# Attention inside a decoder layer: the softmax of each head group cut into six stages, the transposes and products behind it at later weight halves

## The chip, the cores and the metric

The kernel runs on one core of one Trainium2 chip. The metric is the device time of one execution in microseconds (us). Engines are called as in the profile: PE (matmuls; PEld is its weight load), DVE (vector), ACT (scalar activations and copies), POOL and SP (which issues the weight loads).

## What is computed

One decoder layer over 256 tokens of width 2048 in float32: a normalisation, a wide input projection, two token mixers side by side (a recurrent one and attention), their merge, and an MLP. The change touches the attention alone: 32 query heads in 4 groups of 8, each group with one key and value head of 64 columns, a window of 128 tokens in blocks of 128, and one sink per head that takes part in the softmax.

```python
def sliding_window_sink_attention(q, k, v, sinks):
    ...
    scores = jnp.einsum('bnqhgd,bnkhd->bnhgqk', qb, kk).astype(jnp.float32)
    ...
    scores = jnp.where(valid, scores, NEG_INF)
    m = jnp.maximum(jnp.max(scores, axis=-1, keepdims=True), sink)
    p = jnp.exp(scores - m)
    denom = jnp.sum(p, axis=-1, keepdims=True) + jnp.exp(sink - m)
    probs = (p / denom).astype(v.dtype)
    out = jnp.einsum('bnhgqk,bnkhd->bnqhgd', probs, vv)
    return out.reshape(B, S, N_Q_HEADS * HEAD_DIM)
```

## The kernel before

All weights come through one stream (class `Stream`). A chunk of 128x2048 is loaded in two **halves** of 128x1024 (`wraw`, line 76). Each half is split in two float32r parts: ACT casts it to `whi` (line 94), and DVE subtracts that from the original to get `wlo` (line 95). There are 4 raw buffers and 6 of each part, and the split runs 6 halves ahead of the half that PE works on (`AHEAD`). A product takes three matmuls, high by high, low by high and high by low.

For each group `g` of heads there are two passes of PE over the normalised input `hT`, 8 halves each, 12 matmuls of 512 columns per half (`b_pass512`, lines 294, 296, 298): the **g pass** for a gate (banks `g`), then the **q pass** for the queries (banks `q0`, `q1`). The attention of a group is a generator (`attention`, line 532) that the next passes drive: `pump()` runs it up to its next `yield`. `b_pass512` pumps after every `every` halves: the g pass with `every=1`, so 8 times, the q pass with the default 2, so 4 times. The last group has no passes of heads behind it and is driven by the recurrent branch (`a_pair`, lines 254 and 256, tiles `ps`), four times in each pass of four halves. There the wide matmuls have 512 columns and the narrow ones 256.

The generator's stages, in order: rotary embedding of the queries and their transposes for the token blocks 0 and 1 (three stages, tiles `qr`, `pq`, `qT`); the scores; the softmax of block 0; in the next stage that of block 1; then the transposes of the probabilities of block 0 (`turn_probs(0)`, line 604, banks `pt`, copied out by ACT, line 606), an empty stage, those of block 1, and last the outputs (line 630, banks `po`, split by ACT and DVE into `yatt`, lines 634 and 635).

The scores (line 560, banks `sc`) are written in three parts: block 0 with 128 keys per query, and block 1 with 256 keys in two parts `j` = 0 and 1, each in two banks. A bank is emptied by DVE, which scales and masks (line 566, `s`), and then takes the row maxima (line 568, `stat`). In groups 0 to 2 the three parts have banks of their own; in the last group both parts of block 1 use the two banks of pool `psb`, so that the second part waits until the first has been masked. The softmax (lines 571 to 588) takes the maximum with the sink, negates it (575 to 577), computes the exponents on ACT with their sums (line 582, one instruction per head and block), and scales on DVE (lines 584, 585, 587, one instruction for each tile of 512 columns).

A scheduler turns the written order into one static order per engine; matmuls that are wrapped in `pin` keep the order in which they are written among each other. Each engine works off its list strictly in that order, as far as the weight loads of PE are left aside.

## Time and profile before

| | |
|---|---|
| median of 3 runs | 1512.85 us (1512.64 to 1513.12) |
| the profiled execution, its own time | 1512.09 us |
| its span, first to last instruction | 1510.3 us |
| mean granted clock of PE | 0.998 |
| idle time of all engines before the transposes of line 604, put down to the scaling of line 587 | 4.8 us in 5 places |
| casts `whi` (line 94) | 523, mean 1053 ns |
| subtractions `wlo` (line 95) | 523, mean 1221 ns |

In a timeline a row is: start, duration (both us), engine, line, operation, out<-in, shape, count, and in square brackets the idle time of the engine before it with what ended it. Rows with a count merge instructions that follow each other, and then the duration runs from the start of the first to the end of the last. Instructions of one engine overlap a little, so that the distance between two starts is shorter than a duration; where times are added up, starts are used.

The groups follow each other in the trace like this: the q pass of group 1 begins at 106.69 us with group 0's attention beside it, that of group 2 at 160.39 with group 1's, that of group 3 at 215.43 with group 2's, and the recurrent branch at 244.67 with group 3's. The times below that are called those of group 0, 1, 2 or 3 are those of the group whose attention runs. The products with the attention's output (`pp`) begin at 301.24.

### The profile page before, as it was taken

To read this page: it belongs to the slowest core of one execution; us is meant where nothing else is said; L and a number is where in the kernel's file an instruction comes from. 1 tells how busy PE (TensorE), PEld (TensorE's weight loads), DVE (VectorE), ACT (ScalarE), POOL (GpSimd) and SP (SyncE) were. 2 spreads that over 40 slices of the span, in tenths; PEclk is the share of its full clock that TensorE was granted. 3 is DMA by queue.
4 is the path that set the end of the run, shared out by engine and by line. 5 is a ranking of instruction groups with operands and counts; after the bars stand their busy time and mean duration, and the time that the engine had idled before them with its cause. 6 is when DMAs were issued, how large, how long until landed. Compare 5 with 4: busy or idle time off the path is not lost.

```text
span 1510.3 us, 20013 instructions
## 1 busy us (share of the span) xinstructions
PE 1492.1 (99%) x7600; PEld 1260.9 (83%) x7600; DVE 1102.4 (73%) x1379; ACT 829.6 (55%) x1143; POOL 1.7 (0%) x9
## 2 busy tenths in 40 slices
PE   9999999999999999999999999999999999999997
PEld 7887778788888888888888888888888888888886
DVE  6666677858669967555667866698886666789897
ACT  6554654647556766444345655465554555555453
POOL 0000000000000000000000000000000000000000
PEclk9999999999999999999999999999999999999999
DMA  6645445465646565555764756566667665576665
GB/s 254 222 141 188 141 131 172 153 195 167 213 166 212 175 206 196 189 191 187 277 216 140 265 188 193 192 196 213 212 203 237 195 193 188 187 239 210 203 216 187
DMA packets 83327, 296.19 MB, mean 196 GB/s; under 512 B 9760, under 2 KB 10016, under 8 KB 82208
## 3 DMA queue, kind: packets, MB, share of 16 engines
q1 hardware_dynamic: 79920, 287.58, 57.4%
q10 hardware_dynamic: 3312, 7.35, 1.3%
q8 instruction: 59, 0.97, 0.3%
q14 instruction: 36, 0.29, 0.1%
HBM read 288.60 MB, written 6.29 MB: 195 GB/s over the span
## 4 chain that ended last, share of the span: by engine, by line
PE 94%; DVE 4%; ACT 1%; issue 0%; DVEq 0%; ACTq 0%
PE ps L256 22%; PE ps L254 11%; PE dQ L1084 9%; PE s L1084 5%; PE dP L1084 4%; PE pp L294 4%; PE pp L298 4%; PE pp L296 4%; PE dCs L1084 3%; PE g L294 3%; PE g L298 3%; PE g L296 3%; PE q L296 2%; PE q L298 2%; PE q L294 2%; PE o L294 2%
## 5 line engine op out<-in xcount | busy, mean ns | idle before, releaser
L94 ACT CAST whi<-wraw 128x1024 fp32r<-128x1024 f32 x523 | 545.3, 1053 | 566.4 <-PE ps L256 132.3
L95 DVE TENSOR_TENSOR wlo<-wraw,whi 128x1024 fp32r<-128x1024 f32 x523 | 632.7, 1221 | 301.8 <-ACT whi L94 297.9
L256 PE MATMUL ps<-h2T,whi 128*128 128x512 f32 x960 | 223.9, 390 | 0.0
L256 PEld LDWEIGHTS ps<-h2T,whi 128*128 128x128 f32 x960 | 178.3, 188 | 35.5
L256 PE MATMUL ps<-hT,whi 128*128 128x512 f32 x512 | 121.3, 392 | 0.0
L254 PEld LDWEIGHTS ps<-h2T,wlo 128*128 128x128 f32 x960 | 119.2, 192 | 2.3
L254 PE MATMUL ps<-h2T,wlo 128*128 128x256 f32 x960 | 119.9, 283 | 0.0
L256 PEld LDWEIGHTS ps<-hT,whi 128*128 128x128 f32 x512 | 94.7, 188 | 20.1 <-issue 1.5
L1084 PE MATMUL dQ<-whi,uT 128*128 128x512 f32 x288 | 107.0, 389 | 0.0
L294 PE MATMUL g<-whi,hT 128*128 128x512 f32 x256 | 101.3, 396 | 0.0
L296 PE MATMUL g<-wlo,hT 128*128 128x512 f32 x256 | 100.2, 391 | 0.1
L298 PE MATMUL g<-whi,hT 128*128 128x512 f32 x256 | 99.9, 390 | 0.0
L254 PE MATMUL ps<-hT,wlo 128*128 128x256 f32 x512 | 64.9, 284 | 0.0
L254 PEld LDWEIGHTS ps<-hT,wlo 128*128 128x128 f32 x512 | 63.8, 192 | 1.2
L1084 PEld LDWEIGHTS dQ<-whi,uT 128*128 128x128 f32 x288 | 54.1, 188 | 11.2
L294 PEld LDWEIGHTS g<-whi,hT 128*128 128x128 f32 x256 | 48.1, 188 | 10.5 <-issue 1.0
L298 PEld LDWEIGHTS g<-whi,hT 128*128 128x128 f32 x256 | 48.1, 188 | 10.1
L296 PEld LDWEIGHTS g<-wlo,hT 128*128 128x128 f32 x256 | 48.2, 188 | 9.9 <-DVE wlo L95 0.5
L1084 PE MATMUL dQ<-wlo,uT 128*128 128x512 f32 x144 | 56.1, 390 | 0.0
L1084 PE MATMUL dP<-whi,uT 128*128 128x512 f32 x144 | 54.1, 390 | 0.0
L1084 PE MATMUL dCs<-whi,uT 128*128 128x512 f32 x144 | 54.1, 389 | 0.0
L130 DVE TENSOR_TENSOR tlo<-t,thi 128x1536 fp32r<-128x1536 f32 x28 | 49.2, 1756 | 6.4 <-ACT thi L129 6.4
(285 smaller groups left out, 2459.1 us busy)
## 6 DMA issues: line engine op xcount, KB each, us to landing
wraw<-in_w_up SPq DMA_DIRECT2D x128, 512.0 KB, 4.1
wraw<-in_w_dn SPq DMA_DIRECT2D x128, 512.0 KB, 4.7
wraw<-in_w_g SPq DMA_DIRECT2D x64, 512.0 KB, 4.5
wraw<-in_w_xy SPq DMA_DIRECT2D x64, 512.0 KB, 4.5
wraw<-in_w_q SPq DMA_DIRECT2D x32, 512.0 KB, 3.6
wraw<-in_w_ap SPq DMA_DIRECT2D x32, 512.0 KB, 4.7
wraw<-in_w_rp SPq DMA_DIRECT2D x32, 512.0 KB, 4.6
wraw<-in_w_out SPq DMA_DIRECT2D x32, 512.0 KB, 5.0
```

The source lines that it names most:

```text
L94: self.pin(self.nc.scalar.copy(hi, src))
L95: self.pin(self.nc.vector.tensor_tensor(lo, src, hi.bitcast(F32), ALU.subtract))
L130: v.tensor_tensor(lo, t, hi.bitcast(F32), ALU.subtract)
L254: mm(ps[:, f, 1, :], w, a[:, 0, :], start=False, stop=j == 1 and k == 7)
L256: mm(ps[:, f].rearrange("p a b -> p (a b)"), w, a.rearrange("p a b -> p (a b)"), start=kt == 0, stop=j == 3 and k == 7)
L294: mm(banks[tb][n], a[:, 0, t], hi[:, n * 512 : n * 512 + 512], start=first, stop=False)
L296: mm(banks[tb][n], a[:, 0, t], lo[:, n * 512 : n * 512 + 512], start=False, stop=False)
L298: mm(banks[tb][n], a[:, 1, t], hi[:, n * 512 : n * 512 + 512], start=False, stop=last)
L1084: mm(b, a[x], w[y], start=not begun and i == 0, stop=tail and i == 2)
```

## The change

Three things change. The masks and maxima are taken out of `scores` into `masked`, so that the scores of all parts can be written first. `softmax` is cut into `maxima`, `exponents` (for a choice of tiles) and `shares`, and these are spread over six stages. And the q pass now pumps after each of its 8 halves, so that the 13 stages of a group fall on 8 halves of the g pass and the first 5 of the q pass; before, 9 stages fell on 8 halves of the g pass and the first 2 of the q pass.

```diff
@@ scores
+            return tb, j, both
+
+        def masked(tb, j, both):
...
-        def softmax(tb):
+        def maxima(tb):
             stat = stats[tb]
...
+        def exponents(tb, which):
...
+            for k in which:
+                s3, at = tiles[tb][k]
...
+        def shares(tb):
...
-        scores(0, 0, [bank(psm, "sc") for par in range(2)])
-        scores(1, 0, [bank(psb, "sc") for par in range(2)])
+        one = scores(0, 0, [bank(psm, "sc") for par in range(2)])
+        two = scores(1, 0, [bank(psb, "sc") for par in range(2)])
         if not last_group:
-            scores(1, 1, two_banks("sc"))
-        softmax(0)
+            three = scores(1, 1, two_banks("sc"))
+        masked(*one)
+        maxima(0)
+        exponents(0, (0, 1))
         yield
+        masked(*two)
         if last_group:
-            scores(1, 1, [bank(psb, "sc") for par in range(2)])
-        softmax(1)
+            three = scores(1, 1, [bank(psb, "sc") for par in range(2)])
+        yield
+        masked(*three)
+        maxima(1)
+        exponents(1, (0,))
+        yield
+        shares(0)
+        exponents(1, (1,))
+        yield
+        exponents(1, (2, 3))
         yield
         turn_probs(0)
+        shares(1)
         yield
         yield
         turn_probs(1)
+        yield
         yield
...
-        waiting.append(attention(g, b_pass512(hT, [bank(psb, f"q{tb}") for tb in range(TB)])))
+        waiting.append(attention(g, b_pass512(hT, [bank(psb, f"q{tb}") for tb in range(TB)], 1)))
```

Behind line 571 all line numbers of the changed kernel are higher: the masks are line 572, the maxima 574, the exponents 591, the scaling 601, the transposes of the probabilities 618, the outputs 657. `scores` keeps line 560.

The order on PE at the start of the q pass of group 2, with group 1's attention beside it, before:

```order
L298 MATMUL g_1246<-whi47_1304,hT3_136 128x512
L294 MATMUL q0_1529<-whi48_1329,hT0_133 128x512
L604 MATMUL pt_1454<-ident_111,s_1349 128x128 x4
L604 MATMUL pt_1460<-ident_111,s_1349 128x128 x4
L296 MATMUL q0_1529<-wlo48_1330,hT0_133 128x512
```

And now, from the end of the same pass's first half:

```order
L298 MATMUL q0_1486<-whi48_1329,hT0_133 128x512
L294 MATMUL q1_1487<-whi48_1329,hT0_133 128x512
L296 MATMUL q1_1487<-wlo48_1330,hT0_133 128x512
L298 MATMUL q1_1487<-whi48_1329,hT0_133 128x512
L618 MATMUL pt_1506<-ident_111,s_1349 128x128 x4
L618 MATMUL pt_1512<-ident_111,s_1349 128x128 x4
L294 MATMUL q0_1486<-whi49_1388,hT0_133 128x512
```

The transposes of block 0 (of `s_1349`) stood behind the pass's first matmul and stand behind its twelfth. Those of block 1 stand 24 matmuls further now (13 before), in one piece of eight and two of four, and the outputs 20 matmuls behind the last of them (4 before).

The order on ACT in the same place before, `s_1349` being block 0 and `s_1365` block 1:

```order
L94 COPY whi49_1400<-wraw49_1251 128x1024
L94 COPY whi50_1436<-wraw50_1277 128x1024
L94 COPY whi51_1466<-wraw51_1308 128x1024
L578 ACTIVATE stat_1350<-stat_1350 128x8
L582 ACTIVATE s_1349,stat_1350<-s_1349,stat_1350 128x128 x8
L578 ACTIVATE stat_1366<-stat_1366 128x8
L582 ACTIVATE s_1365,stat_1366<-s_1365,stat_1366 128x256 x8
```

And now, where block 1 is called `s_1361`:

```order
L94 COPY whi49_1388<-wraw49_1251 128x1024
L591 ACTIVATE s_1349,stat_1350<-s_1349,stat_1350 128x128 x2
L582 ACTIVATE stat_1350<-stat_1350 128x8
L591 ACTIVATE s_1349,stat_1350<-s_1349,stat_1350 128x128 x6
L94 COPY whi50_1410<-wraw50_1277 128x1024
L591 ACTIVATE s_1361,stat_1362<-s_1361,stat_1362 128x256 x2
L94 COPY whi51_1438<-wraw51_1308 128x1024
L582 ACTIVATE stat_1362<-stat_1362 128x8
L591 ACTIVATE s_1361,stat_1362<-s_1361,stat_1362 128x256 x3
L94 COPY whi52_1462<-wraw52_1333 128x1024
L591 ACTIVATE s_1361,stat_1362<-s_1361,stat_1362 128x256 x3
```

The casts of halves 50 and 51 stood ahead of all exponents; they and the cast of half 52 now stand between them.

The order on DVE in the last group before: `s_2283` is block 0, `s_2299` block 1, `sc_2297` and `sc_2298` the banks of its first part, and `xct` the recurrent branch's convolution (`px`).

```order
L566 TENSOR_SCALAR s_2283<-sc_2282,mask1_422 128x512
L568 TENSOR_REDUCE stat_2284<-s_2283 128x4 x2
L566 TENSOR_SCALAR s_2299<-sc_2297,mask1_422 128x512
L566 TENSOR_SCALAR s_2299<-sc_2298,mask1_422 128x512
L568 TENSOR_REDUCE stat_2300<-s_2299 128x2 x2
L575 TENSOR_TENSOR stat_2284<-stat_2284,sink_418 128x8
L698 TENSOR_SCALAR xct_2162<-px_2163,vec_420,xct_2162 128x255
```

And now, where block 1 is `s_2295` and the banks of its first part are `sc_2293` and `sc_2294`:

```order
L574 TENSOR_REDUCE stat_2284<-s_2283 128x4 x2
L725 TENSOR_SCALAR xct_2162<-px_2163,vec_420,xct_2162 128x255
L579 TENSOR_TENSOR stat_2284<-stat_2284,sink_418 128x8
L725 TENSOR_SCALAR xct_2162<-px_2163,vec_420,xct_2162 128x255
L580 TENSOR_SCALAR stat_2284<-stat_2284 128x8
L725 TENSOR_SCALAR xct_2162<-px_2163,vec_420,xct_2162 128x254
L581 TENSOR_TENSOR stat_2284<-sink_418,stat_2284 128x8
L725 TENSOR_SCALAR xct_2162<-px_2163,vec_420,xct_2162 128x254
L725 TENSOR_SCALAR xct_2162<-px_2163,vec_420,xct_2162 128x253 x2
L95 TENSOR_TENSOR wlo81_2334<-wraw81_2169,whi81_2333 128x1024
L572 TENSOR_SCALAR s_2295<-sc_2293,mask1_422 128x512
L572 TENSOR_SCALAR s_2295<-sc_2294,mask1_422 128x512
```

The masks that empty the banks `sc_2293` and `sc_2294` stood directly behind the maxima of block 0 and stand behind six convolution steps and a weight subtraction. On PE the second part of block 1's scores, which writes these banks again, stood 16 wide matmuls behind the first part and stands 17 wide and 14 narrow ones behind it; between its first and second matmul stands one narrow matmul. Behind the products `pp` every engine's order is as it was.

More of the change, by code (lines that the diff above doesn't have):

```diff
@@ L561, in scores @@
                            kT[r0 : r0 + HD, g, 0:w], start=True, stop=True))
+            return tb, j, both
+        def masked(tb, j, both):
+            w = P * (1 + tb)
+            per = 512 // w
             for par in range(2):
@@ L569, in scores @@
                 tiles[tb].append((s3, at))
-        def softmax(tb):
+        def maxima(tb):
             stat = stats[tb]
-            w = P * (1 + tb)
-            per = 512 // w
             nc.vector.tensor_tensor(stat[:, 0, :], stat[:, 0, :], sk, ALU.max)
@@ L578, in softmax @@
             nc.scalar.activation(stat[:, 2, :], stat[:, 2, :], AF.Exp)
-            for s3, at in tiles[tb]:
+        def exponents(tb, which):
+            stat = stats[tb]
+            per = 512 // (P * (1 + tb))
+            for k in which:
+                s3, at = tiles[tb][k]
                 for i in range(per):
@@ L583, in softmax @@
                                          accum_out=stat[:, 3, c])
+        def shares(tb):
+            stat = stats[tb]
+            w = P * (1 + tb)
+            per = 512 // w
             nc.vector.tensor_tensor(stat[:, 2, :], stat[:, 2, :], stat[:, 3, :], ALU.add)
```

## The prediction

> **What bounds the kernel now.** I read the page first, then PE's waits, then the tile of the transposes, then the timelines of PE, DVE and ACT around them. The page's first lines:

> ```profile
> span 1510.3 us, 20013 instructions
> PE 1492.1 (99%) x7600; PEld 1260.9 (83%) x7600; DVE 1102.4 (73%) x1379; ACT 829.6 (55%) x1143; POOL 1.7 (0%) x9
> ```

> PE is the bound, so the change can only win time in which PE stands still. PE's waits by line, and for the tile of the transposes what its engine's idle time ended on (us, times):

> ```profile
> PE pt L604 <- DVE s L587: 4.4, 3, 1.5
> ...
>   DVE s L587: 4.8, 5
> ```

> The only large wait is that of the probability transposes (L604) for the scaled probabilities (L587): 4.8 us in five places. Idle time is counted from the modelled end of the matmul before, so I measure from start to start instead. PE's timeline at the first transposes of group 0, of group 1, of group 1's last transposes (nothing to wait for), and of group 2:

> ```profile
> 108.05 0.39 PE L294 MATMUL q<-whi,hT 128*128 128x512 f32 x1
> 108.49 1.23 PE L604 MATMUL pt<-ident,s 128*128 128x128 f32 x8
> 109.48 0.47 PE L296 MATMUL q<-wlo,hT 128*128 128x512 f32 x1
> ...
> 160.39 0.39 PE L294 MATMUL q<-whi,hT 128*128 128x512 f32 x1
> 162.20 1.23 PE L604 MATMUL pt<-ident,s 128*128 128x128 f32 x8 [1.42 <-DVE s L587]
> 163.19 0.48 PE L296 MATMUL q<-wlo,hT 128*128 128x512 f32 x1
> ...
> 168.53 0.39 PE L298 MATMUL q<-whi,hT 128*128 128x512 f32 x1
> 168.77 1.03 PE L604 MATMUL pt<-ident,s 128*128 128x128 f32 x8
> 169.56 0.47 PE L294 MATMUL q<-whi,hT 128*128 128x512 f32 x1
> ...
> 217.24 1.23 PE L604 MATMUL pt<-ident,s 128*128 128x128 f32 x8 [1.42 <-DVE s L587]
> ```

> Undisturbed, the matmul ahead takes 0.24 us and eight transposes 0.79. In group 1 these are 1.81 and 0.99: 1.57 + 0.20 = 1.77 us lost (the 0.20 is the second bank, which waits for the second scaled tile). Group 2 repeats it, 1.77; group 0 loses 0.20 + 0.20 = 0.40. The last group works beside the next stage's passes:

> ```profile
> 258.71 3.92 PE L256 MATMUL ps<-hT,whi 128*128 128x512 f32 x16
> 262.56 1.14 PE L560 MATMUL sc<-kT,qT 64*128 64x256 f32 x8
> ...
> 267.80 1.32 PE L256 MATMUL ps<-hT,whi 128*128 128x512 f32 x5
> 270.66 0.63 PE L604 MATMUL pt<-ident,s 128*128 128x128 f32 x4 [1.54 <-DVE s L587]
> ...
> 277.72 2.19 PE L254 MATMUL ps<-hT,wlo 128*128 128x256 f32 x17
> 280.01 0.63 PE L604 MATMUL pt<-ident,s 128*128 128x128 f32 x4
> ...
> 293.98 4.00 PE L254 MATMUL ps<-hT,wlo 128*128 128x256 f32 x32
> 297.81 3.59 PE L256 MATMUL ps<-hT,whi 128*128 128x512 f32 x15
> ```

> A 256-column matmul steps at (297.81 - 293.98) / 32 = 0.12 us, and I take 0.227 for 512 columns. Five from 267.80 end at 268.94, the transposes start at 270.66: 1.70 lost with a little slack; 17 from 277.72 end at 279.76, start 280.01: 0.25. **What can be won is 0.40 + 1.77 + 1.77 + 1.95 = 5.9 us**, no more.

> **The change part by part.** No arithmetic is added or removed: the same masks, exponents, scalings, transposes and products run, and behind the last group the order on every engine is as before. PE's number of switches between passes and attention work stays too (eight in each of groups 0 to 2, ten in the last). So the sum is waits removed less waits added.

> *Groups 0 to 2, block 0.* Where the transposes stood one matmul (seven in group 0) into the q pass, they now stand twelve in: 2.72 us after its start, 163.11 in group 1. When are the probabilities ready? DVE and ACT of group 1 today, with the PE matmul that the cast waits for, and two copies of group 2:

> ```profile
> 148.85 1.28 DVE L566 SCALAR_TENSOR_TENSOR s<-sc,mask 128x512 f32<-128x512 f32 x2
> 152.01 0.39 PE L298 MATMUL g<-whi,hT 128*128 128x512 f32 x1
> 152.43 1.06 ACT L94 CAST whi<-wraw 128x1024 fp32r<-128x1024 f32 x1 [4.76 <-PE g L298]
> 156.07 1.21 DVE L95 TENSOR_TENSOR wlo<-wraw,whi 128x1024 fp32r<-128x1024 f32 x1
> 157.20 0.16 DVE L576 TENSOR_SCALAR stat<-stat 128x8 f32<-128x8 f32 x1
> 157.71 0.39 ACT L582 ACTIVATE s<-s,stat 128x128 f32<-128x128 f32 x1
> 160.90 0.49 ACT L582 ACTIVATE s<-s,stat 128x256 f32<-128x256 f32 x1
> 161.37 1.29 DVE L587 TENSOR_TENSOR s<-s,stat 128x512 f32<-128x512 f32 x2
> ...
> 224.81 1.07 ACT L606 COPY pT<-pt 128x512 f32<-128x512 f32 x2
> ```

> Twelve masks and reductions and a small operation fill DVE from 148.85 to 156.07: 0.595 each. A wlo takes 1.13 (156.07 to 157.20), a scaling 0.6, eight short exponents with one of the sinks 3.2 on ACT (157.71 to 160.90), a long one 0.49, and a cast whi 0.95, since the last 0.1 of an operation lies beside the next one, as the pairs show. Today the twelve and a wlo go ahead of the negated maximum at 157.20. Now the negated maximum of block 0 stands behind six of them: 148.85 + 6 x 0.595 + 0.2 = 152.7, so its exponents end at 152.7 + 3.2 = 155.9. DVE ends its twelve at 156.3, then scales, subtracts one wlo and scales: both tiles ready at 159.4, against 163.11. **Slack 3.7 us; the wait goes.** The same steps give 105.7 against 109.4 in group 0.

> *Groups 0 to 2, block 1.* ACT now has casts between the exponents: from 155.9 whi, 2 exponents, whi, 3, whi, 3: 3 x 0.95 + 8 x 0.49 + 0.3 = 7.1, so 163.0. DVE sums, inverts and scales three tiles by 165.3, the fourth behind a wlo by 167.0. PE is there 24 matmuls behind the first transposes, at 163.11 + 1.0 + 5.6 = 169.7. Slack again. A new small wait is likely: ACT's cast starts 0.42 us after the start of the twelfth matmul of a half (152.01, 152.43) and takes 0.95; behind it stand the two copies out of the transposes' banks, 0.57 the first, so a bank is free some 1.94 us after that start; PE asks for it after 0.32 + 0.79 + three matmuls with the switch, 0.77, at 1.88. I take 0.1 us per group; the bounds are 0 and one copy, 0.5.

> *The weights.* Today ACT casts at 152.43 in group 1 and again 2.72 later; now these two wait until 155.9 and 158.0. Their wlo follow at 158.6 and 160.5, and PE needs them at 166.9 and 170.6 by the order. Cover is 8 us; if it were gone, a late half would stop PE for what it is late. SP's loads wait for the raw buffers that wlo frees; wlo comes within 1.7 us of today's time or earlier, so no load lands late.

> *The last group.* Here one wait goes and another comes. The scores of block 1's second half write the same two banks that its first half's masks have to empty. DVE today:

> ```profile
> 258.81 1.28 DVE L566 SCALAR_TENSOR_TENSOR s<-sc,mask 128x512 f32<-128x512 f32 x2
> 261.20 1.27 DVE L566 SCALAR_TENSOR_TENSOR s<-sc,mask 128x512 f32<-128x512 f32 x2
> 263.65 0.48 DVE L698 SCALAR_TENSOR_TENSOR xct<-px,vec,xct 128x255 f32<-128x255 f32 x1
> 266.17 1.21 DVE L95 TENSOR_TENSOR wlo<-wraw,whi 128x1024 fp32r<-128x1024 f32 x1
> 267.30 1.28 DVE L566 SCALAR_TENSOR_TENSOR s<-sc,mask 128x512 f32<-128x512 f32 x2
> ```

> These masks run at 261.20 today and the scores follow at 262.56 without a wait. In the new order six convolution steps and a wlo go ahead of them: 261.20 + 2.55 (263.6 to 266.17) + 1.13 = 264.9; the first mask has written at 265.6, the second at 266.2. PE is at the scores 17 wide and 14 narrow matmuls after 258.71: 262.65 + 1.7 + 0.1 = 264.5. It waits 1.15 us, does one, and waits 0.2 for the other bank: **1.35 us new**, and a narrow matmul between them costs one switch more, 0.2. Behind the waiting scores PE queues the rest of the pass. No row of before shows such a wait: bounds 0 (today's case) and 2.8 (if the reductions too had to be over, 267.3).

> Block 0's transposes then come at 276.3. DVE on the way there: masks to 266.1, reductions, xs, wlo, masks, reductions, two wlo, the next pass's px at 274.1, two scalings: 275.5 and 276.1. Just in time. Block 1: exponents end at 278.35, scalings at 279.4, 282.4, 283.0 and 284.2; PE asks at 281.5, 283.3 and 284.3, and each time finds them by 0.1 to 2 us. Copies may hold the banks: 0.25 (bounds 0 and 1). One switch fewer among the transposes: -0.1. So the last group loses 1.35 + 0.2 + 0.25 - 0.1 = 1.7, having lost 1.95.

> **Sum:** -5.9 + 3 x 0.1 + 1.7 = -3.9 us. The profiled execution took 1512.09 (span 1510.3 and 1.8 around it), so it would take 1508.2; the median of the runs is 0.76 higher, so **1509.0**, 0.26% less.

> [...] The clock over group 1's wait (window, us, busy of PE, PEld, DVE, ACT, POOL, granted clock, DMA):

> ```profile
> 160.00:176.00 16.00, 14.58 (x75) 9.97 (x74) 10.45 (x16) 13.89 (x37) 0.00 (x0) 1.00 0.38 129
> ```

> It stays at 1.00, so a wait costs its own length. [...]

> **The rivals.**
> 1. *The last group's wait grows.* Its chain runs with 0.1 to 0.2 us in hand at three places. For it: the masks stand behind everything that DVE does in these rows. At the upper bounds (2.8 for the scores, 1 us for the copies) and 0.3 more in each other group: -5.9 + 1.2 + 3.9 = -0.8; halfway between this and the forecast is 1510.5, no change that counts. 28%.
> 2. *Slower: the weights run late.* Exponents now stand between casts, and a cast also frees the way for the raw buffer's next load. If the casts of a q pass fell 8 us behind, which is the cover above, each further delay would stop PE; one half late by one half's time, 2.72 us, in each of three groups: -3.9 + 8.2 = +4.3, 1517.1. For it: ACT is busy for 13.89 of the 16 us of the window row. Against it: the exponents now begin at 152.7, where ACT comes out of 4.76 us of idleness (row 152.43). 7%.
> 3. *The clock.* If matmuls behind each of three waits of 1.8 us ran at half pace for as long, 0.9 each would be won on top: -6.6, 1506.2. The row of 1.00 is against it. 2%. [...]
> 4. *The change does less than it says*, the transposes standing too early still: the order has them twelve matmuls in, so I give it nothing of its own beyond rival 1.

> **How the numbers follow.** The forecast (-3.1 to -5.9) has 63%. A difference of 0.2%, 3.0 us, is about what a measurement here can tell from none; the forecast and rival 3 lie beyond it: faster 0.65, same 0.28, slower 0.07. The range goes from 1506.9 (nothing new waits) up into rival 1, 1512.0; above it lie its worst part and rival 2.

> **What would show it.** In PE's waits the line of the transposes on the scaled probabilities should fall from 4.4 to under 0.5, and a line of the scores (L560) on the masks of 1 to 1.5 us, once, should be new. From the start of the q pass beside each of groups 0 to 2 to the first transposes 2.7 us should pass. Wrong would be: transposes of block 1 that wait for ACT's copies or for scalings for more than 0.5 us, a wait on wlo, or a last group that loses over 3 us.

## The result, and the profile after

The changed kernel takes 1510.39 us (median of 20 runs, 1509.16 to 1512.35), the kernel before on the same chip 1512.7 (20 runs, 1512.1 to 1513.78). The ratio is 0.9985, with a 95% interval of 0.9979 to 0.9991. A second series on another occasion gave 0.9986 (0.9977 to 0.9995). So the change wins about 2.2 us, 0.15%, where 3.9 were forecast, and lies just inside the 0.2% that the prediction set as the bound of what counts.

The profiled execution took 1509.99 us, forecast 1508.2. Its page begins:

```profile
span 1508.2 us, 20012 instructions
PE 1492.7 (99%) x7600; PEld 1261.5 (84%) x7600; DVE 1101.7 (73%) x1379; ACT 828.7 (55%) x1143; POOL 1.7 (0%) x9
```

The span is 2.1 us shorter at the same work. PE's waits by line between 90 and 300 us, and from the tile of the transposes what the idle time of PE, its weight load (PEld) and ACT ended on, and who waited for the tile (us, times):

```profile
PE sc L560 <- DVE s L572: 1.1, 1, 1.1
...
  ACT pT L620: 2.0, 4
...
  DVE s L601: 0.4, 1
...
  PEld pt L618: 2.0, 4
```

The transposes' line of 4.4 us is gone. One wait of the scores on the masks is new, once, and the copies out of the transposes' banks now hold up PE's weight load in four places, once in each group. These 2.0 us are idle time of the weight load; what the matmuls lose by it is less, and is measured below. PE's order is simple enough here to compare stage by stage. The table gives the distance between the first matmul of a stage and that of the next one, in us; it is free of what happens ahead of the stage.

| stage | before | after | forecast of the difference | measured |
|---|---|---|---|---|
| q pass beside group 0 | 27.90 | 27.73 | -0.30 | -0.17 |
| q pass beside group 1 | 29.24 | 27.77 | -1.67 | -1.47 |
| q pass beside group 2 | 29.24 | 27.77 | -1.67 | -1.47 |
| the recurrent pass beside the last group, up to `pp` | 56.57 | 56.86 | -0.25 | +0.29 |
| sum | | | -3.9 | -2.8 |

Of the 2.8, PE still has 2.5 at the start of its last matmul (1500.3 before, 1497.8 after). The span is only 2.1 shorter, since what follows that matmul, the last vector steps and the store of the output, took 0.4 longer in this execution.

**The q passes.** PE in the q pass of group 2, with group 1's attention beside it: its start, the transposes of block 0, and those of block 1.

```profile
160.28 0.39 PE L294 MATMUL q<-whi,hT 128*128 128x512 f32 x1
...
162.77 0.39 PE L298 MATMUL q<-whi,hT 128*128 128x512 f32 x1
163.00 1.03 PE L618 MATMUL pt<-ident,s 128*128 128x128 f32 x8
163.79 0.47 PE L294 MATMUL q<-whi,hT 128*128 128x512 f32 x1
...
169.13 0.39 PE L298 MATMUL q<-whi,hT 128*128 128x512 f32 x1
169.36 1.03 PE L618 MATMUL pt<-ident,s 128*128 128x128 f32 x8
...
170.70 0.40 PE L298 MATMUL q<-whi,hT 128*128 128x512 f32 x1
171.19 0.66 PE L618 MATMUL pt<-ident,s 128*128 128x128 f32 x4
171.60 0.48 PE L294 MATMUL q<-whi,hT 128*128 128x512 f32 x1
```

The first eight transposes come 2.72 us after the pass's start, and take 0.79: undisturbed, as forecast. DVE had scaled the second tile by 159.0, where 159.4 was forecast. The next eight, at 169.36, do not wait either. The third set should stand 0.23 behind the matmul of 170.70 and stands 0.49 behind it: 0.26 lost. ACT shows what it waits for, a bank that the first of two copies still reads:

```profile
169.60 1.05 ACT L94 CAST whi<-wraw 128x1024 fp32r<-128x1024 f32 x1 [1.67 <-PE q L298]
170.56 1.06 ACT L620 COPY pT<-pt 128x512 f32<-128x512 f32 x2
```

A weight cast starts 0.24 us behind the transposes' start and the copies stand behind it. The first copy, half of the row, is over near 171.1, and the transposes follow. With 0.06 more inside the set that is 0.32 per group (0.29 in group 0).

**The last group.** PE and then DVE at the second part of block 1's scores:

```profile
259.65 1.83 PE L254 MATMUL ps<-hT,wlo 128*128 128x256 f32 x14
262.61 0.70 PE L560 MATMUL sc<-kT,qT 64*128 64x256 f32 x2 [1.13 <-DVE s L572]
263.24 0.38 PE L254 MATMUL ps<-hT,wlo 128*128 128x256 f32 x1
263.55 1.13 PE L560 MATMUL sc<-kT,qT 64*128 64x256 f32 x6
264.61 2.29 PE L254 MATMUL ps<-hT,wlo 128*128 128x256 f32 x17
```

```profile
260.74 1.22 DVE L95 TENSOR_TENSOR wlo<-wraw,whi 128x1024 fp32r<-128x1024 f32 x1
261.88 1.28 DVE L572 SCALAR_TENSOR_TENSOR s<-sc,mask 128x512 f32<-128x512 f32 x2
```

The first of the 14 starts at 259.65, so the last is over at 259.65 + 14 x 0.12 = 261.33, and the scores start at 262.61: 1.3 us. From there to the narrow matmuls it takes 2.00, of which 0.11 is the matmul between; before, the eight scores took 1.06 (262.56 to 263.62). So 0.8 more, for the second bank and the switch. The DVE rows are the chain that was forecast: weight subtraction, then the masks.

### The profile page after: what moved, and what is told of

Same layout as the page of the kernel before. It is cut to its first block, busy times and chain, and to the rows that moved or that the text cites. A ratio compares the mean times of both kernels' runs of the same rounds, so it can differ in the third digit from the quotient of the medians.

```text
span 1508.2 us, 20012 instructions
## 1 busy us (share of the span) xinstructions
PE 1492.7 (99%) x7600; PEld 1261.5 (84%) x7600; DVE 1101.7 (73%) x1379; ACT 828.7 (55%) x1143; POOL 1.7 (0%) x9
## 4 chain that ended last, share of the span: by engine, by line
PE 84%; DVE 8%; DMA 4%; ACT 2%; issue 1%; DVEq 0%; SPq 0%; ACTq 0%
PE ps L256 21%; PE ps L254 11%; PE dQ L1111 5%; PE pp L298 4%; PE pp L294 4%; PE pp L296 4%; PE g L294 4%; DMA wraw<-in_w_dn 4%; PE g L298 4%; PE g L296 4%; DVE wlo L95 3%; PE s L1111 3%; PE dP L1111 2%; PE q L294 2%; PE q L298 2%; PE q L296 2%
## 5 line engine op out<-in xcount | busy, mean ns | idle before, releaser
L95 DVE TENSOR_TENSOR wlo<-wraw,whi 128x1024 fp32r<-128x1024 f32 x523 | 632.7, 1221 | 306.1 <-ACT whi L94 302.9
L94 ACT CAST whi<-wraw 128x1024 fp32r<-128x1024 f32 x523 | 544.2, 1052 | 554.0 <-PE ps L256 127.3
L256 PE MATMUL ps<-h2T,whi 128*128 128x512 f32 x960 | 223.9, 390 | 0.0
L256 PEld LDWEIGHTS ps<-h2T,whi 128*128 128x128 f32 x960 | 178.3, 188 | 35.6
L256 PE MATMUL ps<-hT,whi 128*128 128x512 f32 x512 | 121.3, 392 | 0.0
L254 PEld LDWEIGHTS ps<-h2T,wlo 128*128 128x128 f32 x960 | 119.1, 192 | 2.3
L254 PE MATMUL ps<-h2T,wlo 128*128 128x256 f32 x960 | 119.9, 283 | 0.0
L256 PEld LDWEIGHTS ps<-hT,whi 128*128 128x128 f32 x512 | 94.7, 188 | 19.8 <-issue 1.1
L294 PE MATMUL g<-whi,hT 128*128 128x512 f32 x256 | 101.3, 396 | 0.0
L296 PE MATMUL g<-wlo,hT 128*128 128x512 f32 x256 | 100.1, 391 | 0.1
L298 PE MATMUL g<-whi,hT 128*128 128x512 f32 x256 | 99.9, 390 | 0.0
L254 PEld LDWEIGHTS ps<-hT,wlo 128*128 128x128 f32 x512 | 63.7, 192 | 1.8 <-issue 0.7
L254 PE MATMUL ps<-hT,wlo 128*128 128x256 f32 x512 | 64.7, 284 | 0.0
L294 PEld LDWEIGHTS g<-whi,hT 128*128 128x128 f32 x256 | 48.1, 188 | 10.5 <-issue 1.0
L296 PEld LDWEIGHTS g<-wlo,hT 128*128 128x128 f32 x256 | 48.1, 188 | 10.1 <-DVE wlo L95 0.5
L298 PEld LDWEIGHTS g<-whi,hT 128*128 128x128 f32 x256 | 48.1, 188 | 10.1
```

Source lines behind the costliest of these rows:

```text
L94: self.pin(self.nc.scalar.copy(hi, src))
L95: self.pin(self.nc.vector.tensor_tensor(lo, src, hi.bitcast(F32), ALU.subtract))
L254: mm(ps[:, f, 1, :], w, a[:, 0, :], start=False, stop=j == 1 and k == 7)
L256: mm(ps[:, f].rearrange("p a b -> p (a b)"), w, a.rearrange("p a b -> p (a b)"), start=kt == 0, stop=j == 3 and k == 7)
L294: mm(banks[tb][n], a[:, 0, t], hi[:, n * 512 : n * 512 + 512], start=first, stop=False)
L296: mm(banks[tb][n], a[:, 0, t], lo[:, n * 512 : n * 512 + 512], start=False, stop=False)
```

## The experiments

They ran in three series (1 to 4, 5 to 8, 9 and 10), each beside the kernel before on the same chip (1513.12, 1513.35 and 1513.43 us). Single executions spread by some 3 us, from the arrival of the first loads (the first q pass starts at 59.1 to 60.1 us) and from the store at the end (the span ends 9.95 to 11.8 us behind the start of PE's last matmul). Where less than that is asked, the distance from the first q pass's start to the first `pp` is used: 242.14 and 242.15 in two profiles of the kernel before, 239.29 in the changed kernel.

**1. The same kernel again.**

> The changed kernel once more, for its spread. My account: PE's time from the first q pass with attention beside it to the products behind the last group is 2.7 us shorter than before, in every execution, so the median stays 2 to 2.8 us below before; the 3 us between its lowest and highest time would then come from behind the attention, where the order of every engine is as before. Rival: the spread comes from the attention itself, from waits that depend on when weights land; then a profile of a slower execution shows waits there that the first profile does not have.

1511.37 us (1509.47 to 1513.2), ratio 0.9986. Its profile holds something that the first one did not. Each row is one stretch of 3.41 us around the scores' wait (busy time of PE, PEld, DVE, ACT, POOL, then the granted clock and the DMA):

```profile
257.83:261.24 3.41, 3.41 (x22) 3.06 (x22) 3.41 (x11) 2.57 (x9) 0.00 (x0) 1.00 0.00 0
261.24:264.65 3.41, 2.28 (x12) 1.24 (x10) 3.41 (x6) 3.23 (x12) 0.00 (x0) 1.00 0.40 117
264.65:268.07 3.42, 3.42 (x17) 3.41 (x17) 3.42 (x6) 0.00 (x0) 0.00 (x0) 0.50 0.28 91
268.07:271.48 3.41, 3.41 (x17) 2.86 (x17) 2.01 (x5) 1.05 (x1) 0.00 (x0) 1.00 0.45 163
```

Directly behind the wait the clock stands at 0.50 for 3.41 us, and the narrow matmuls step by 0.213 us in place of 0.12. The waits are those of the first profile, but the recurrent pass takes 58.38 us in place of 56.86: 1.5 more. The distance to `pp` is 240.81. So neither account holds: the median is 1.75 below the kernel before, not 2 to 2.8; 1.5 us of this execution's extra time arose inside the attention; and no wait is longer than in the first profile. It is the clock.

**2. The later place alone.** The old softmax stages, with the q pass pumped after each half and four empty stages, so that transposes and outputs stand where the change puts them:

```diff
+        yield
+        yield
+        yield
         turn_probs(0)
         yield
         yield
         turn_probs(1)
+        yield
         yield
...
-  b_pass512(hT, [bank(psb, f"q{tb}") for tb in range(TB)])
+  b_pass512(hT, [bank(psb, f"q{tb}") for tb in range(TB)], 1)
```

> The kernel before with its whole softmaxes, but the transposes and outputs at the stages of the changed kernel (three empty stages ahead of the first transposes, one ahead of the outputs, the q pass pumping after each half). My account (what counts is that the transposes stand later; cutting the softmax only adds the wait of the last group's scores): the waits on the scaled probabilities go, the scores of the last group wait for nothing, and copies cost up to 0.7 us in each of groups 1 to 3: 3.7 us less than before, some 0.9 less than the changed kernel. Rival (the staged softmax is what makes the probabilities ready in time): transposes still wait over 1 us in groups 1 and 2, and the gain is under 1.5 us.

1510.47 us (1509.36 to 1512.1), ratio 0.9983. PE's waits:

```profile
PE pt L604 <- ACT pT L606: 2.1, 3, 0.9
PE pt L604 <- DVE s L587: 0.5, 1, 0.5
```

In groups 0 to 2 block 0's transposes wait for nothing, so it is the later place that removes the old waits; the cut of the softmax into stages is not needed for that. What the cut adds is time in hand: in group 1 the second scaled tile is done at 162.6 here, 0.5 us ahead of the transposes, and in the changed kernel 4 us ahead. But the copies cost more than in the changed kernel: the q passes take 27.64, 28.32 and 28.32. Here is why, block 0 (the first row) and block 1 in group 1:

```profile
163.06 1.03 PE L604 MATMUL pt<-ident,s 128*128 128x128 f32 x8
...
169.42 1.03 PE L604 MATMUL pt<-ident,s 128*128 128x128 f32 x8
170.21 0.48 PE L294 MATMUL q<-whi,hT 128*128 128x512 f32 x1
171.29 1.14 PE L604 MATMUL pt<-ident,s 128*128 128x128 f32 x8 [0.60 <-ACT pT L606]
```

Block 1's second eight ask for the banks one matmul behind the first, three in the changed kernel, and the copies are done at about the same time in both. So they wait 0.85 us (171.29 - 170.21 - 0.23). The last group takes 56.49. The distance to `pp`, 239.94, is 0.65 above the changed kernel's; the forecast was 0.9 below.

**3. The last group's masks one stage earlier.**

```diff
         exponents(0, (0, 1))
+        if last_group:
+            masked(*two)
         yield
-        masked(*two)
+        if not last_group:
+            masked(*two)
```

> The changed kernel, but in the last group the first part of block 1 is masked one stage earlier, right behind block 0. My account: the 1.3 us wait of the last group's scores for the masks is a real loss of PE and goes, with the extra switch: 1.4 to 1.5 us less than the changed kernel, and the later transposes of that group wait no more than 0.6 us as now. Rival (the wait only moves: DVE's chain to block 0's transposes is as late as before): the transposes of block 0 wait instead, and the time stays within 0.5 us of the changed kernel.

1510.07 us (1508.75 to 1510.98), ratio 0.9977. The scores' wait is gone, and another has come:

```profile
PE pt L618 <- DVE s L601: 1.0, 2, 0.5
```

The recurrent pass takes 56.27, only 0.6 less than in the changed kernel. The account, 1.4 to 1.5, fails, and the rival is near: it had the wait move to block 0's transposes and the time stay within 0.5. PE is early now at the transposes, by what it no longer lost at the scores, and DVE, busy for 24.25 of the 25 us from 258 to 283, is late there with the scaled tiles. So the wait was worth 2.1 us where it stood, and 0.6 in the end.

**4. That, and block 1's transposes in two stages,** so that ACT has a half's time for the copies between:

```diff
-        turn_probs(1)
+        turn_probs(1, (0,))
+        yield
+        turn_probs(1, (1,))
         yield
-        yield
```

> As mask_early, and the transposes of block 1 are cut into two stages, so that the second eight stand twelve matmuls behind the first eight. My account: the waits on ACT's copies (0.3 us in each of groups 0 to 2, 0.6 in the last) go as well: 2.4 to 2.8 us less than the changed kernel, 5.2 to 5.6 less than before. Rival (the copies are late because ACT is, and the second eight wait there too): no better than mask_early.

1508.28 us (1507.63 to 1509.37), ratio 0.9968 (0.9957 to 0.998), the lowest median of all. The q passes take 27.43, 27.45 and 27.45: the 0.3 of each group is gone, which shows that it was the copies' banks. The recurrent pass takes 56.00, and the distance to `pp` is 237.49: 1.8 below the changed kernel, where 2.4 to 2.8 was expected, and 4.65 below the kernel before. What is missing is the scores' wait, which is again worth far less than its length. What is left in front of the last group's transposes is again DVE:

```profile
PE pt L620 <- DVE s L601: 1.0, 2, 0.5
```

**5. The last group's transposes one stage later still,** in that kernel:

```diff
         yield
+        if last_group:
+            yield
         turn_probs(0)
```

> The kernel of both (in the last group the masks of block 1's first part one stage earlier, the transposes of block 1 cut in two stages) with one more empty stage in the last group ahead of block 0's transposes, so that they and all that follows stand one recurrent half later. Theory: what both still loses in the last group, about 1.5 us in front of the transposes, is the time that DVE is late with the scaled probabilities, and a later place takes it away as the later place took the waits of groups 0 to 2 away. Then PE waits nowhere for attention, the run is about 1.5 us below both, near 1506.8, 6 us below the kernel before, and no execution shows a granted clock under 0.998. Rival: DVE is busy all the time in this stretch, so that the wait only moves on to the outputs or to the products behind the group: then the time is that of both within 0.3 us.

1508.79 us (1508.28 to 1510.08), ratio 0.9968. The recurrent pass takes 56.71, 0.7 more than without the extra stage. PE:

```profile
272.07 1.04 PE L620 MATMUL pt<-ident,s 128*128 128x128 f32 x8
...
280.93 0.87 PE L620 MATMUL pt<-ident,s 128*128 128x128 f32 x6 [1.30 <-DVE s L601]
...
288.75 1.08 PE L665 MATMUL po<-s,v_sb 128*64 128x512 f32 x4 [0.74 <-ACT pT L622]
```

Block 0's transposes wait no more, but block 1's do, and the outputs as well. The theory of a cure by a later place fails here, and the rival's mechanism holds: the scaled tiles stand behind the recurrent branch's own vector work on a full DVE (busy for all of the 10 us from 275 to 285), and the wait moves on. By the ratios the time is that of experiment 4, as the rival has it; the distance to `pp`, 238.24, is 0.75 longer, more than its 0.3.

**6. The old stages for the last group, the new ones for the others.**

> The changed kernel for groups 0 to 2, with the stages of the kernel before for the last group. Theory: the last group is worse off by the change, by 0.3 us at the end of its stage (56.57 us before, 56.86 after) and by more where the clock falls behind the wait of its scores; with the old stages it loses what it lost before, and the run is 0.3 us below the changed kernel, -3.1 against the kernel before, and its profile has the wait of 1.5 us in front of the last group's first transposes back. Rival: the last group's loss depends on when groups 0 to 2 end, and the wait of the old stages is longer or shorter here: then it differs from the changed kernel by more than 0.3 us in either direction.

1510.12 us (1508.9 to 1511.94), ratio 0.9979. The recurrent pass takes 56.58, as in the kernel before (56.57), with its old wait:

```profile
267.86 0.63 PE L618 MATMUL pt<-ident,s 128*128 128x128 f32 x4 [1.54 <-DVE s L601]
```

The distance to `pp` is 239.04, 0.25 below the changed kernel, as the theory said: in the last group the new stages lose 0.3 more than the old ones, in two profiles whose clock does not fall there.

**7. The kernel before again.**

> The kernel before once more, for its profile and for the granted clock of each of its executions. Theory: a fall of the clock to half for some 3.4 us behind a wait of over a microsecond is a thing that both kernels have in some executions; here too a part of the executions then shows a mean granted clock of 0.997 or less and is 1 to 2 us longer than those at 0.998. Rival: only the changed kernel has it, by its scores' wait, and here nearly all executions stand at 0.998. Ratio 1.000 either way.

1514.02 us (1512.2 to 1514.75), ratio 1.0. Its profile has no fall of the clock inside the program. But the mean clock of an execution turned out to be a poor witness between 0.997 and 0.998: the clock also falls once PE has ended, and this tail alone, 5 to 8.5 us at half, gives 0.997 to 0.998 in the profiles without any other fall. A mean of 0.996 takes 10.5 us or more at half, longer than any of these tails, and so points to one more fall; but a fall of 3.41 us ahead of a short tail still shows as 0.997. At 0.996 or less stand 5 of 86 listed executions of the kernel before and 1 of 31 of the changed kernel, and for the changed kernel that is a lower bound. So the expectation was formed on a measure that cannot carry it. That the kernel before has falls at all is not shown: neither of its two profiles holds one.

**8. The masks ahead of the release computed twice.**

> The changed kernel, with the two masks of block 1's first part in the last group each computed twice into the same place: 1.2 us more of DVE between the maxima and the release of the banks for which the last group's scores wait. The static order sets these scores six narrow matmuls, 0.7 us, later. Theory: the scores wait for the masks, and behind them the scaled probabilities come 1.2 us later: the two together cost 0.9 to 1.3 us, so 0.9 to 1.3 above the changed kernel in executions with an undisturbed clock. If a longer wait also makes the clock fall more often, the granted clock is 0.997 or less in most executions and the median is 2 to 3 us above the changed kernel. Rival: DVE has time in hand there, and the cost is under 0.4 us.

1511.62 us (1509.4 to 1513.8), ratio 0.9985. The distance to `pp` is 239.08, 0.2 below the changed kernel: the theory of 0.9 to 1.3 fails, and the rival, under 0.4, holds for PE. In the trace 25 narrow matmuls stand ahead of the scores, where the changed kernel has 14: eleven more, 1.3 us, and not the six that were expected. So PE comes later by what DVE is later, and the scores wait as long as before:

```profile
PE sc L560 <- DVE s L573: 1.1, 1, 1.1
```

Nor do the transposes wait longer for the scaled tiles (0.3 us, once, in their tile's list; 0.4 in the changed kernel), so DVE had made the 1.2 us good by then (the changed kernel's DVE still stands idle for 1.27 us at 275). Still 5 of 11 executions stand at 0.996 or less, against 1 of 31. The profile itself holds no fall; the last section comes back to it.

**9 and 10. A longer wait in a fixed order.** The recurrent pass's matmuls behind the scores are kept in the order in which they are written, so that the scheduler cannot put others ahead of the waiting scores; in the second kernel the masks are also computed three times. The theory counts in windows of 3.41 us, the length of the stretch at 0.50 in experiment 1, and takes one that PE leaves mostly empty to be followed by one at half clock; how empty it must be is the author's estimate, and no run shows it.

```diff
+                if hold["on"]:
+                    pin(m)
...
             three = scores(1, 1, [bank(psb, "sc") for par in range(2)])
+            hold["on"] = True
...
+        hold["on"] = False
         turn_probs(0)
```

> The changed kernel, but with the recurrent pass's matmuls of the last group kept in their written order behind the scores, so that the scores stand right behind 16 wide matmuls: the 14 narrow and one wide matmul that the scheduler had put ahead of them come after them. DVE releases the banks when it did, so the scores wait 1.9 us longer, 3.2 in all. [...] With 3.2 us of wait and 1.7 us of half empty scores one window is that empty for more than half of the phases that the grid can have: most executions have a fall, the median is 1.9 + 1.2 to 1.7 above the changed kernel, and in the profile the fall, if there is one, begins exactly at the end of the window that covers most of the wait. Rival: a wait costs its own length: 1.9 above the changed kernel, and granted clocks of 0.997 to 0.998 as there.

> As hold_x1, with the two masks ahead of the release each computed three times into the same place, so that the scores wait 2.4 us longer again, 5.6 us in all, in the same order on PE. Theory of the windows: however the grid lies, one window has at least 2.8 of its 3.41 us empty, so that every execution has a fall, and some have two: granted clock 0.997 or less in every execution and 0.996 or less in most, 2.4 + 0 to 0.5 us above hold_x1, 6 us above the changed kernel. Rival: the wait costs its own length and no more, 4.3 above the changed kernel, with the granted clocks of the changed kernel.

They take 1514.05 us (1512.43 to 1516.19, ratio 1.0006, 0.9997 to 1.0015) and 1518.07 (1515.46 to 1519.61, ratio 1.003, 1.0021 to 1.0039). The waits are 3.2 us, as planned, and 6.3, for 5.6; 10 of 11 and 10 of 10 executions stand at 0.996 or less. First the first kernel, in the windows that the clock's own changes mark, then the second:

```profile
259.04:262.46 3.42, 0.72 (x4) 0.26 (x2) 3.42 (x9) 2.65 (x15) 0.00 (x0) 1.00 0.00 0
262.46:265.87 3.41, 3.08 (x9) 2.24 (x10) 3.41 (x7) 2.14 (x6) 0.00 (x0) 0.50 0.48 154
265.87:269.28 3.41, 3.41 (x17) 3.31 (x17) 1.80 (x3) 0.00 (x0) 0.00 (x0) 0.50 0.00 0
269.28:272.70 3.42, 3.42 (x25) 3.16 (x25) 3.42 (x10) 0.91 (x4) 0.00 (x0) 1.00 0.55 165
```

```profile
258.67:262.08 3.41, 1.25 (x6) 0.71 (x4) 3.41 (x10) 2.65 (x13) 0.00 (x0) 1.00 0.00 0
262.08:265.49 3.41, 0.00 (x0) 0.00 (x0) 3.41 (x7) 2.67 (x9) 0.00 (x0) 0.50 0.47 154
265.49:268.91 3.42, 2.88 (x9) 2.06 (x10) 3.35 (x8) 0.00 (x0) 0.00 (x0) 0.50 0.00 0
268.91:272.32 3.41, 3.41 (x16) 3.31 (x16) 3.37 (x6) 0.00 (x0) 0.00 (x0) 0.50 0.00 0
```

Each fall begins at the end of a window that PE left empty for the most part (busy for 0.72 and 1.25 us of 3.41), and in all three falls seen the clock comes back at the end of the first window that PE fills (busy for 3.42, 3.41 and 3.41 us in experiments 1, 9 and 10). The recurrent pass takes 60.92 and 63.91 us: 4.06 and 7.05 more than in the changed kernel, of which the longer waits are 1.9 and 5.0. The rest, 2.1 in both, arises where the rows show the clock at 0.50; the theory had 1.2 to 1.7 and 1.7 for it, estimates that no run shows. The rival, that a wait costs its own length, fails.

## Why the prediction was right and where it was not

- **What bounds the kernel, and what can be won.** Right. PE is the bound, and with all waits gone (experiment 4) a q pass takes 27.44, so that the old losses were 0.46, 1.80 and 1.80, forecast 0.40, 1.77 and 1.77.
- **Groups 0 to 2, block 0.** Right, by its own test: 2.72 us from the pass's start to the first transposes, and no wait. The chain on DVE came as forecast too (both tiles at 159.0 for 159.4). Experiment 2 adds that the place does it, and that the stages only add time in hand.
- **Block 1, the copies' wait.** The right wait in the right place, mis-sized: 0.1 was taken, 0.3 came, three times (0.65 us of the miss, of which the larger old losses give 0.12 back). The step took a bank to be free 1.94 us and PE to ask for it 1.88 after the twelfth matmul of a half, a difference of 0.06 between two sums of rounded terms. The rows after give 171.19 - 169.13 = 2.06 and 170.93 - 169.13 = 1.80. The bounds, 0 and 0.5, held.
- **The weights.** Right. No wait on `wlo` came up; rival 2 did not happen.
- **The last group.** Mechanism and place right, three terms too small. The scores' wait for the first bank was forecast as 1.15 and is 1.3; the second bank and the switch were 0.4 and are 0.8; the transposes, 0.25 for the copies, lose 0.5. About half of that 0.5 is not the copies': at 280.7 the weight load of four transposes waited 0.44 us for a scaled tile, where the prediction had each tile found ready. Together 2.6 for 1.8. The old loss was larger too, by small gaps at the other transposes that the prediction left out: about 2.2 for 1.95. So the stage lost 0.29 where it was to win 0.25. This is rival 1 in part: its place and its cause, a third of its price.
- **The sum and the chances.** The median, 1510.39, lies inside the range, but the 2.3 us won lie short of the forecast's own bounds (-3.1 to -5.9, given 63%); the outcome is no change that counts, which had 28%. -3.9 was forecast, -2.8 came out on PE and -2.1 in the span of one execution, -2.3 in the medians. What lies between -2.8 and -2.3 is smaller than the spread of the runs, and its cause is open. The same holds for the share of the medians that is due to falls of the clock: 30 of the changed kernel's 31 executions stand at 0.997 or 0.998, where a fall cannot be told from the tail.
- **The clock.** Here the prediction was wrong. It read a clock of 1.00 over group 1's wait and concluded that "a wait costs its own length". The reading was true of that wait, and nothing was to be won back there, so rival 3 fell rightly; its 0.9 us for each wait is shown by no run, and over the three old waits the clock stands at 1.00 (160 to 176, 215 to 230 and 250 to 275 us in the kernel before). The conclusion was too wide: the new wait of the scores did cost the clock in one of two profiles, 1.5 us on top of its own length, and by the mean clock in nearly every execution once it was made longer (20 of 21 at 0.996 or less in experiments 9 and 10). The two waits differ by what stands in the window with them, as the last section argues; the prediction did not ask what the new one would do to the clock.

Experiments 3 to 5 also show what the forecast's form left out: the last group's waits are one budget. PE and a full DVE work beside each other for some 25 us, and a wait taken away at the scores comes back by two thirds at the transposes.

## What to carry to other kernels

Where the engine that is waited for is full, price a wait at the end of the stretch and not where it stands: the 2.1 us at the scores were worth 0.6. A difference of less than 0.1 us between two chains worked out from rounded rows decides nothing, so take half of the bound for it and not a token. And a wait on PE has to be read with its neighbours: ask how little work the emptiest 3.4 us around it hold (27, 16 and 32% ahead of the three falls inside the programs here, by the count of the last section), and look at the granted clock in the profiles of more than one execution.

## What the runs showed of the hardware

How empty a window must be is not settled by these runs. Counted in matmul time at an even pace (0.227 us for 512 columns, as they step in the trace, and half of it, 0.113, for all narrower ones, an estimate, where those of 256 columns step by 0.12; two scores that start 7 ns apart as one), the falls inside followed windows with 27, 16 and 32% of work, and those at the programs' ends windows with 35% or less. The emptiest windows in the attention at full clock that no fall followed had 46 to 50%: in the kernel before those with the old wait of 1.57 us, in experiment 8 the one with the new wait. But the first windows behind the first full clock, at the programs' start, had only 38 to 43% in five profiles (there PE was busy for 2.15 to 2.29 of the 4.00 us from 4 to 8), and no fall followed them. And undisturbed scores step by 0.21 us for 256 columns, not by 0.113 (0.209 in the kernel before); counted at that pace the window of experiment 1 holds 43%, as much as those. (Should a record be missing, its window would seem emptier than it was.) So the runs show falls behind nearly empty windows and none behind half full ones, but no limit between them.

The grid explains the chance in it. The changed kernel's stretch of wait and scores is some 3.3 us long, from 261.3 to 264.6. In experiment 1 one window covers it exactly (261.24 to 264.65); in the first profile of the changed kernel the grid cuts it at 262.80, and both windows keep 57% of work and more. The grid's place against the program differs from one execution to the next: the first full clock comes 4.4 to 6.9 us after the first instruction.

The length of the idleness alone does not decide: 1.3 us of idleness beside the scores were enough in one of three profiles that hold them, while 1.57 us among full matmuls were not, and neither were 1.85 us between 4 and 8 us in experiment 4.

Why experiment 8, whose wait is no longer, shows 5 of 11 executions at 0.996 or less and the changed kernel 1 of 31 can in part be worked out, as an estimate that no run tests. The grid that covers the scores also places the fall behind PE's end. In experiment 1 that fall comes 4.1 us behind the start of the last matmul (1499.6 and 1503.69). With the 9.95 to 11.8 us from there to the end, an execution with a fall at the scores then has 9.3 to 11.1 us at half in all, a mean of 0.997 in most cases. In experiment 8 the scores stand 1.5 us later, so the window that covers them ends later too, and counted on in steps of 3.413 us the last fall comes some 2.7 us behind the last matmul's start: 10.7 to 12.5 us at half, a mean of 0.996. So a fall at the scores shows in the mean clock there and mostly does not in the changed kernel, and the two counts do not say that falls are more frequent in experiment 8. How often the changed kernel's clock falls stays open.
